# Weight tiles before the MLP split by DMAs on GpSimd's queue, and the RG-LRU's directions summed by a DMA

## The chip, the cores and the metric

The kernel runs on one core of a Trainium2 chip. The metric is the device time of one execution in microseconds. Before the change three runs took 1648.96, 1650.98 and 1652.66 us; the median is 1650.98. The profile was taken of one further execution.

## What is computed

One layer of a hybrid backbone over 1024 latent tokens and 256 context tokens, width 1024, all in float32:

```python
rgx, gate, s5u = split(modulate(x, sh1, sc1) @ w_in)        # [1024, 3 * 1024], context likewise
xc   = centred_dwconv(rgx)                                  # width 4
h_f, h_b = rglru(xc, forward), rglru(xc, backward)          # 8 heads, gates of 128x128, linear scans
rg   = (h_f + h_b) * gelu(gate)
y    = s5(s5u, forward) + s5(s5u, backward) + d * s5u       # 64 groups, complex diagonal state of 64
g    = gelu(y);  s5 = g * sigmoid(g @ glu_w + glu_b)
out  = concat(rg, s5) @ w_out + b_out
x1   = layer_norm(alpha * x + g1 * out)
x2   = layer_norm(alpha * x1 + g2 * (relu(modulate(x1, sh2, sc2) @ w1 + b1) ** 2 @ w2 + b2))
```

The scans of the latents start from the last state of the context's scan in the same direction.

## The kernel before

Channels lie on the 128 partitions and tokens along the free axis. Every float32 product is made of three products of float32r parts: a weight tile `w` and an input `x` are each written as a high and a low part, and PE takes high by high, high by low and low by high. The function `weights` (line 101) makes the parts of one weight tile of 128 x 1024 (512 KB): SP loads the raw tile into a buffer of tag `wr`, ACT casts it to the high part `wh`, and DVE subtracts to get the low part `wl`. Each of the three tags has three buffers. All weights of the two-dimensional products pass through it.

```python
raw = wp.tile([P, 1024], F32, tag="wr", name="wr", bufs=3)
ld(raw, src)
S.copy(hi, raw)
tt(lo, raw, f(hi), SUB)
```

The program is one long straight line in stages, without loops on the chip. `tc` plans the order on every engine's queue beforehand; an engine then works through its queue in order and waits there for what an instruction needs. `after(ins)` puts instructions behind `ins` on an engine's queue.

1. Start. The modulations are computed, the inputs are modulated and split, and the first two tiles of the input projection (`wrg`) are multiplied along with that. The parameters of S5 are computed on DVE.
2. The mixer's inner part, in an order written out by hand as letters: G is a tile of the RG-LRU's input projection (`proj_rgx`), S one of S5's (`proj_s5`), R a head of the RG-LRU (`rg_head`), X and T are S5's matrices (`make_xt`, `s5_taps`). G and S call `project` (line 359), which takes a weight tile and makes 72 products of it. A head convolves a row on DVE (`xc`), ACT rounds it to `xch`, DVE makes `xcl`, PE makes the gates (`ps_g`), ACT takes sigmoid, exponential, tanh and root, and DVE scans both directions. Then DVE adds the backward scan to the forward one, and SP (GpSimd for head 7) stores the sum as `hs`.
3. `s5_in` makes what each chunk of tokens adds to the state. `proj_gate` makes the eight gate tiles: `project`, GELU, load of `hs`, product, store as `mx`. Two scans over the chunks (`scan`) run on DVE as chains of small operations.
4. The first half of the output projection takes the stored tiles `mx` (`mix_in`). For five of them the low part is already made as the change does it for weights: ACT writes the negated high part, and a DMA on GpSimd's queue adds the raw tile to it. `k_outer` multiplies two weight tiles at once, channel by channel, for tiles 0 and 1 and again for 6 and 7; tiles 2 to 5 go one by one through `prod` (48 products a tile).
5. S5's outputs (`s5_out`): ACT and DVE copy the states that the chunks start from (`s5_states`), PE multiplies, ACT takes GELU (`gs`). The GLU has eight weight tiles, the first two in `k_outer` along with `s5_out`, the others one by one. The other modulations (`mods`) are loaded by SP as `mo` and multiplied on DVE here and in the next stage.
6. The second half of the output projection, 16 steps: eight weight tiles for the first 512 tokens, and the same eight again for the others, 24 products a step. SP also loads the partial sum and the input into a `pin` buffer, which shares the tag `wr`. The first norm runs on DVE beside it.
7. The MLP with the second norm. Its weights go through `weights` and `weights2`.

For stages 5 and 6 the raw tiles were asked for two tiles ahead, through the list `ahead` (lines 816 and 958).

Of the kernel before, what the change touches and what calls it, by code (L numbers as in the profile page):

```python
# [15 lines left out]
P = 128  # L16
# [25 lines left out]
def build(nc, tc, a, out):  # L42
# [51 lines left out]
    def split_affine(h, lo, t, x, scale, bias, behind=None):  # L94
        # h + lo = scale * x + bias; t is for the part of it that h leaves
        with after(behind):
            S.activation(h, x, AF.Identity, bias=bias, scale=scale)
        S.activation(t, f(h), AF.Identity, bias=bias, scale=-1.0)
        stt(lo, x, scale, t, MUL, ADD)
# [45 lines left out]
    def mods1(k0, n):  # L145
        # shift and scale of the channel tiles k0 to k0 + n, both of latents and context
# [108 lines left out]
    # lambda to the powers 8, 16, .. 128, as re, im, -im  # L255
# [13 lines left out]
    # softplus(-lambda), times 8  # L269
# [87 lines left out]
    alt = [0]  # L357

    def project(m, ctx, evict, behind=None, load=None):
        wh, wl = weights(a["w_in"][m], load)  # L360
# [17 lines left out]
    # a row of the convolution's input: context at 1, latents at 260, zeros around them  # L378
    RGW = 1 + NC + 2 + 1 + NL + 2

    def proj_rgx(m):
# [8 lines left out]
        if m < 2:  # L390
            for i, ps in enumerate(early[m]):
                evict(i, ps)
        else:
            project(m, True, evict)
# [4 lines left out]
    def rg_head(h, xr):  # L399
# [28 lines left out]
        # a = exp(-s), s = 8 softplus(-lambda) r; 1 - a^2 = tanh(s / 2) (1 + a)^2  # L428
        # (each function for both directions at once: the tables change thrice a head)
# [20 lines left out]
        tt(it[0][:, NC:NT], it[0][:, NC:NT], it[1][:, NC:NT], ADD)  # L450
        d = dr.tile([P, NL], F32, name=f"hs{h}")
        (nc.sync if h < 7 else G).dma_start(out=d, in_=it[0][:, NC:NT])
        hsum[h] = d

# [8 lines left out]
    def proj_s5(m):  # L463
# [8 lines left out]
        project(16 + m, True, evict)  # L472
# [4 lines left out]
    def make_x(g0, n):  # L477
        # X[(d, p), g, (t, ci)]
# [27 lines left out]
    def s5_taps(m):  # L506
# [9 lines left out]
        # tap 0 of both directions and the skip  # L516
# [46 lines left out]

    rxs = [proj_rgx(0), proj_rgx(1)]
    step = {"R": lambda m: rg_head(m, rxs[m]), "G": lambda m: rxs.append(proj_rgx(m)), "S": proj_s5, "X": make_xt, "T": s5_taps}
    for o in ('X0 R0 T0 G2 S0 R1 X1 S1 T1 R2 X2 G3 S2 T2 R3 G4 X3 T3 X4 R4 T4 S3 G5 R5 X5 S4 G6 X6 T5 R6 G7 X7 S5 T6 R7 T7 S6 S7').split():
        step[o[0]](int(o[1:]))
# [30 lines left out]
    def scan(hf):  # L598
        h = H[hf]
        hs = slice(hf * GH, (hf + 1) * GH)  # L600
        # the context's chunks in pairs, pairs of pairs ..: its last state in the last of its chunks
# [21 lines left out]
    def proj_gate(m):  # L623
# [8 lines left out]
        project(8 + m, False, evict, last_in[m] if m else None, in_ld[m - 2] if m >= 2 else None)  # L632
# [42 lines left out]
    def k_outer(ws, xs, tags, name, ks_=range(KT)):  # L675
        # some tiles of a product at once, over the channels as they come
# [16 lines left out]
    for m, pss in enumerate(k_outer([weights(a["w_out"][0, m]) for m in range(2)], mix_next, ("rg", "si"), "ps_wo")):  # L693
        put_part(m, pss)
    for m in range(2, 6):
        w = weights(a["w_out"][0, m])
# [5 lines left out]
    for m, pss in enumerate(k_outer([weights(a["w_out"][0, m]) for m in (6, 7)], lambda k: mix[k], ("rg", "mm"), "ps_wo",  # L702
# [5 lines left out]
    sop.append(pool("so1", stack=sost))  # L708
    wglu = [weights(a["glu"][m]) for m in range(2)]

    def starts(H, h2, g, cp):
        # the states that the chunks start from, in the chunks' own order
# [42 lines left out]
    for hf in range(2):  # L755
# [6 lines left out]
        # their place is that of the states  # L762
# [53 lines left out]
    ahead = [weights(a["glu"][m]) for m in range(2, 2 + 2)]  # L816
    for m in range(8):
        if m > 1:
            if m + 2 < 8:
                ahead.append(weights(a["glu"][m + 2]))  # L820
            w = ahead.pop(0)
# [21 lines left out]
    def mean_of(pl, x, n):  # L843
        # the mean over all channels of tiles whose sum is x, on every partition
# [4 lines left out]
    def rsqrt(v, t):  # L849
        # v to the power -1/2 in t[0], t[1] is taken as well; the engines' roots are refined by a step of Newton's  # L850
# [7 lines left out]
    def rstd_of(pl, n, tag, sq):  # L858
        # 1 / standard deviation on every partition, from the sum of the tiles' squares
# [15 lines left out]
    def normalise(pl, ys, n, tag, done):  # L875
        """ys less their mean over the channels, over their standard deviation, in place; done(m) after each. In steps."""
# [24 lines left out]
    def centre(n):  # L901
        """Tiles, sent in one by one, less their mean over the channels, in place. In steps."""
# [15 lines left out]
    def scale(pl, n, tag, done, end):  # L918
        """Tiles of no mean, sent in one by one, over their standard deviation, in place; done(m) after each. In steps."""
# [38 lines left out]
    ahead = [weights(a["w_out"][1, m]) for m in range(2)]  # L958
    for j in range(2):
        ys = []  # L960
        for m in range(8):
            if 8 * j + m + 2 < 16:
# [260 lines left out]
```

## Time and profile before

| | |
|---|---|
| runs | 1648.96, 1650.98, 1652.66 us, median 1650.98 |
| span of the profiled execution | 1648.7 us (the page gives no other time of its own; it is 2.3 us below the median) |
| PE busy | 1557.3 us, 94% |
| DVE busy | 1109.4 us, 67% |
| ACT busy | 711.3 us, 43% |
| GpSimd (POOL) busy | 8.8 us, 1% |
| bytes moved by DMA | 199.27 MB, 121 GB/s over the span |

Times are in microseconds from the start of the span. An engine is busy while an instruction of its own runs; the profile says of idle time what ended it. A DMA has two times: what its issue takes on the queue, and the time from issue to landing. The DMA share is the mean busy share of the sixteen DMA engines. PEclk is TensorE's granted clock as a share of 2.4 GHz, so 0.50 is 1.2 GHz.

### The profile page before, as it was taken

The numbers are of one execution on the slowest core, as the hardware profiler recorded it, in microseconds if no ns is written. First come the engines' busy times: TensorE is split into PE (matmuls) and PEld (weight loads), VectorE is DVE, ScalarE is ACT, GpSimd is POOL, SyncE is SP. The second block draws the span as 40 slices with busy tenths as digits, with TensorE's granted clock in tenths as the row PEclk, the third lists the DMA queues.
The fourth block names the chain that finished last, engine by engine and source line by source line (L and its number), as shares of the span: only waits on it lengthen the run. The fifth ranks groups of instructions, "written<-read, shape, count | busy, mean of one in ns | idle before, by whom it ended". The sixth has DMA issues, their size and how long they took to land.

```text
span 1648.7 us, 20069 instructions
## 1 busy us (share of the span) xinstructions
PE 1557.3 (94%) x7508; PEld 1271.8 (77%) x7508; DVE 1109.4 (67%) x2371; ACT 711.3 (43%) x978; POOL 8.8 (1%) x37
## 2 busy tenths in 40 slices
PE   7899998999879999799999899999999999999997
PEld 2687777777758787697778688888888888888887
DVE  7999899998939899329878853343432334247856
ACT  4666667666792326744335642113130303031225
POOL 0000000000000100000000000000000000000000
PEclk9999999999999999899999899999999999999998
DMA  8533323333745836965686422112110202022202
GB/s 268 204 118 112 105 104 115 124 115 108 255 151 167 237 132 149 230 166 196 202 280 184 168 86 72 39 39 64 52 52 17 73 13 90 13 77 84 70 1 103
DMA packets 92721, 199.27 MB, mean 121 GB/s; under 512 B 12496, under 2 KB 43728, under 8 KB 91472
## 3 DMA queue, kind: packets, MB, share of 16 engines
q1 hardware_dynamic: 77424, 176.10, 34.1%
q10 hardware_dynamic: 14048, 17.70, 3.1%
q0 software_dynamic: 1152, 4.19, 1.1%
q8 instruction: 59, 0.97, 0.2%
q14 instruction: 38, 0.31, 0.1%
HBM read 153.98 MB, written 43.98 MB: 120 GB/s over the span
## 4 chain that ended last, share of the span: by engine, by line
PE 62%; DVE 19%; DMA 8%; ACT 6%; issue 4%; SPq 0%; ACTq 0%; DVEq 0%; POOLq 0%
PE ps_m L665 22%; PE ps_m L1052 21%; PE ps_g L425 3%; PE ps_mm L370 3%; PE ps_wo L665 3%; DMA mo<-in_ada_t 2%; PE ps_wo L684 2%; DVE xc L56 2%; DVE ii L47 2%; DVE wl L47 2%; ACT H L593 1%; DVE mo L56 1%; PE ps_gl L684 1%; DVE rr L56 1%; DVE ii L445 1%
## 5 line engine op out<-in xcount | busy, mean ns | idle before, releaser
L665 PE MATMUL ps_m<-x,wh 128*128 128x512 f32 x1024 | 324.8, 398 | 7.8 <-DVE yb L47 7.8
L665 PEld LDWEIGHTS ps_m<-x,wh 128*128 128x128 f32 x1024 | 193.8, 189 | 55.9 <-issue 8.4
L1052 PE MATMUL ps_m<-hh,w2h 128*128 128x512 f32 (+1 forms) x576 | 211.3, 368 | 0.0
L1052 PE MATMUL ps_m<-hl,w2h 128*128 128x512 f32 (+1 forms) x576 | 210.9, 366 | 0.0
L1052 PE MATMUL ps_m<-hh,w2l 128*128 128x512 f32 (+1 forms) x576 | 210.9, 366 | 0.0
L665 PE MATMUL ps_m<-x,wl 128*128 128x512 f32 x512 | 204.1, 399 | 0.0
L47 DVE TENSOR_TENSOR acc<-ps_m,acc 128x512 f32<-128x512 f32 (+1 forms) x144 | 90.8, 631 | 141.5 <-PE ps_m L1052 140.7
L90 ACT CAST wh<-wr 128x1024 fp32r<-128x1024 f32 x88 | 92.2, 1051 | 212.9 <-PE ps_m L665 102.5
L47 DVE TENSOR_TENSOR wl<-wr,wh 128x1024 fp32r<-128x1024 f32 x88 | 107.4, 1222 | 106.9 <-ACT wh L90 106.6
L370 PE MATMUL ps_mm<-x0h,wh 128*128 128x512 f32 x352 | 140.5, 399 | 1.0 <-ACT wh L90 1.0
L370 PE MATMUL ps_mm<-x0h,wl 128*128 128x512 f32 x352 | 140.5, 400 | 0.9 <-DVE wl L47 0.9
L370 PE MATMUL ps_mm<-x0l,wh 128*128 128x512 f32 x352 | 140.2, 398 | 0.0
L1034 ACT CAST w2h<-wr 128x1024 fp32r<-128x1024 f32 x28 | 28.7, 1051 | 237.2 <-PE ps_m L1052 206.5
L1052 PEld LDWEIGHTS ps_m<-hh,w2h 128*128 128x128 f32 x576 | 108.6, 189 | 18.4 <-ACT hh L1015 0.6
L1052 PEld LDWEIGHTS ps_m<-hl,w2h 128*128 128x128 f32 x576 | 108.6, 189 | 18.0 <-issue 0.5
L1052 PEld LDWEIGHTS ps_m<-hh,w2l 128*128 128x128 f32 x576 | 108.6, 189 | 17.7 <-issue 0.2
L665 PEld LDWEIGHTS ps_m<-x,wl 128*128 128x128 f32 x512 | 97.0, 189 | 23.8 <-issue 0.2
L47 DVE TENSOR_TENSOR r<-r 128x512 f32<-128x512 f32 x64 | 44.3, 692 | 84.3 <-ACT hh L1015 83.4
L1014 ACT ACTIVATE r<-ps_m,cols 128x512 f32<-128x512 f32 x64 | 43.8, 685 | 99.3 <-PE ps_m L665 91.9
L665 PE MATMUL ps_wo<-ms,wh 128*128 128x512 f32 x256 | 79.9, 392 | 1.6 <-DVE ms L47 1.2
L370 PEld LDWEIGHTS ps_mm<-x0h,wl 128*128 128x128 f32 x352 | 67.3, 191 | 14.4 <-DVE wl L47 1.4
L370 PEld LDWEIGHTS ps_mm<-x0h,wh 128*128 128x128 f32 x352 | 67.2, 191 | 13.6 <-ACT wh L90 1.4
(295 smaller groups left out, 2989.6 us busy)
## 6 DMA issues: line engine op xcount, KB each, us to landing
wr<-in_w SPq DMA_DIRECT2D x64, 512.0 KB, 3.6
mo<-in_ada_t SPq DMA_DIRECT2D x32, 512.0 KB, 4.0
wr<-in_w_in SPq DMA_DIRECT2D x24, 512.0 KB, 4.2
wr<-in_w_out SPq DMA_DIRECT2D x24, 512.0 KB, 4.5
xt<-xt ACTq DMA_DIRECT2D x16, 512.0 KB, 2.7
yd<-Y SPq DMA_DIRECT2D x16, 512.0 KB, 2.6
xt<-xt SPq DMA_DIRECT2D x16, 512.0 KB, 5.2
yf<-yd SPq DMA_DIRECT2D x8, 1024.0 KB, 9.5
```

The lines of the kernel that those rows point to most:

```text
L47: (eng or V).tensor_tensor(out=o, in0=x, in1=y, op=op)
L56: V.scalar_tensor_tensor(out=o, in0=x, scalar=s, in1=y, op0=op0, op1=op1, **kw)
L90: S.copy(hi, raw)
L370: PE.matmul(ps, w[:, ks], x, start=(k == 0 and c == 0), stop=(k == KT - 1 and c == 2))
L425: PE.matmul(ps, w[:, w0:w0 + P], x[:, src:src + n], start=(c == 0), stop=(c == 2))
L445: V.tensor_tensor_scan(out=i, data0=q, data1=i, initial=0.0, op0=MUL, op1=ADD)
L593: S.copy(hv[0:64], ps[0:64])
L665: PE.matmul(ps, u[:, ks], v[:, js], start=(c == 0), stop=(c == 3 * KT - 1))
L684: PE.matmul(ps, u[:, ks], v[:, HS[j]], start=(i == 0 and c == 0), stop=(i == KT - 1 and c == 2))
L1014: S.activation(r, ps, AF.Relu, bias=col("b1", i))
L1034: S.copy(hi, raw)
L1052: PE.matmul(ps, w[:, m * P:(m + 1) * P], x[:, js], start=(c == 0), stop=(c == 3 * bk - 1))
```

## The change

The 54 weight tiles from the third tile of the input projection to the end of the output projection no longer go through `weights`. They stand in one list `wseq` in the order of use. `fetch` loads a tile straight into a high-part buffer by a DMA on GpSimd's queue that casts float32 to float32r. `lower` writes the negated high part on ACT into a low-part buffer and adds the raw tile to that by a second DMA on GpSimd's queue, which reads the tile from HBM again. `take` hands out the next tile and asks for later ones: the low part of the next tile and the high part of the one after it. The high and low parts still have three buffers each. The first two tiles and the MLP's keep `weights`. The forward scan of a head is stored by SP, and a DMA on GpSimd's queue adds the backward scan to it in HBM; DVE's addition is gone.

```diff
+    wseq, whl = [], []
+    def fetch(n):
+        while len(whl) < min(n, len(wseq)):
+            hi = wp.tile([P, 1024], F32R, tag="wh", name="wh", bufs=3)
+            G.dma_start(out=hi, in_=wseq[len(whl)])
+            whl.append([hi, None])
+    lows = [0]
+    def lower(n):
+        while lows[0] < min(n, len(wseq)):
+            i = lows[0]
+            fetch(i + 1)
+            lo = wp.tile([P, 1024], F32R, tag="wl", name="wl", bufs=3)
+            S.activation(lo, f(whl[i][0]), AF.Copy, scale=-1.0)
+            G.dma_start(out=lo, in_=wseq[i], accum_op=ADD)
+            whl[i][1] = lo
+            lows[0] += 1
+    used = [0]
+    def take(ahead=1):
+        i = used[0]
+        used[0] += 1
+        lower(i + 1)
+        fetch(i + 2)
+        lower(i + 1 + ahead)
+        fetch(i + 2 + ahead)
+        return whl[i]
...
-    def project(m, ctx, evict, behind=None, load=None):
-        wh, wl = weights(a["w_in"][m], load)
+    def project(ctx, evict, behind=None):
+        wh, wl = take()
...
-        tt(it[0][:, NC:NT], it[0][:, NC:NT], it[1][:, NC:NT], ADD)
         d = dr.tile([P, NL], F32, name=f"hs{h}")
-        (nc.sync if h < 7 else G).dma_start(out=d, in_=it[0][:, NC:NT])
+        ld(d, it[0][:, NC:NT])
+        G.dma_start(out=d, in_=it[1][:, NC:NT], accum_op=ADD)
...
+    wseq += [a["w_in"][int(o[1:]) + (16 if o[0] == "S" else 0)] for o in order if o[0] in "GS"]
+    wseq += [a["w_in"][8 + m] for m in range(8)] + [a["w_out"][0, m] for m in range(8)]
+    wseq += [a["glu"][m] for m in range(8)] + [a["w_out"][1, m % 8] for m in range(16)]
+    fetch(2)
+    lower(1)
     rxs = [proj_rgx(0), proj_rgx(1)]
...
-    for m, pss in enumerate(k_outer([weights(a["w_out"][0, m]) for m in range(2)], mix_next, ("rg", "si"), "ps_wo")):
+    for m, pss in enumerate(k_outer([take(), take(0)], mix_next, ("rg", "si"), "ps_wo")):
...
-        w = weights(a["w_out"][0, m])
+        w = take()
...
-    wglu = [weights(a["glu"][m]) for m in range(2)]
+    wglu = [take(), take(0)]
...
-            if m + 2 < 8:
-                ahead.append(weights(a["glu"][m + 2]))
-            w = ahead.pop(0)
+            w = take()
...
-            if 8 * j + m + 2 < 16:
-                ahead.append(weights(a["w_out"][1, (m + 2) % 8]))
-            w = ahead.pop(0)
+            w = take()
```

## Rows read from the trace of the kernel before

**Rows 1.** The page: busy time of each engine over the span.
```profile
PE 1557.3 (94%) x7508; PEld 1271.8 (77%) x7508; DVE 1109.4 (67%) x2371; ACT 711.3 (43%) x978; POOL 8.8 (1%) x37
```

**Rows 2.** Windows, stage A and one head: length, engines' busy time, PEclk, DMA share, GB/s.
```profile
core 0: us, PE busy (x) PEld busy (x) DVE busy (x) ACT busy (x) POOL busy (x), PEclk, DMA share, GB/s
153.50:198.00 44.50, 42.18 (x224) 35.11 (x223) 39.40 (x54) 29.16 (x39) 0.17 (x3) 0.96 0.32 110
109.40:410.00 300.60, 281.91 (x1520) 233.65 (x1520) 281.79 (x372) 199.54 (x263) 0.85 (x15) 0.97 0.32 109
```

**Rows 3.** PE's waits, 105 to 412 us: total, times, longest.
```profile
PE ps_g L425 <- ACT xch L411: 13.8, 6, 3.0
```

**Rows 4.** Windows, the chunk scans.
```profile
490.00:640.00 150.00, 144.76 (x620) 118.00 (x620) 141.82 (x705) 46.04 (x59) 4.39 (x5) 0.98 0.54 162
```

**Rows 5.** Tile `wl` on DVE, 490 to 640 us: duration in ns, first and last start.
```profile
L47 DVE TENSOR_TENSOR wl<-wr,wh x15: 1211/1218/1222, 493.4 to 637.6; 128x1024 fp32r<-128x1024 f32 x15
```

**Rows 6.** Timeline of ACT: the first copy of states, and what it waited for.
```profile
637.61 2.09 ACT L714 COPY h<-H 64x1024 f32<-64x1024 f32 x1 [3.93 <-DVE H L47]
```

**Rows 7.** PE's waits, 540 to 700 us.
```profile
PE ps_so L741 <- ACT gs L744: 11.7, 1, 11.7
```

**Rows 8.** Windows, stage F.
```profile
822.00:904.00 82.00, 80.46 (x360) 65.93 (x360) 65.63 (x108) 31.34 (x41) 0.00 (x0) 1.00 0.70 225
```

**Rows 9.** Tile `ms`: stage F's products with the high part of the weights.
```profile
L665 PE MATMUL ps_wo<-ms,wh x256: 387/389/796, 812.4 to 905.9; 128*128 128x512 f32 x128
```

**Rows 10.** DMA, 810 to 908 us: SP's queue (share of 98 us), and loads' time to landing.
```profile
q1 hardware_dynamic: 9502, 21.70, 69.0%
...
wr<-in_w_out SPq DMA_DIRECT2D x12, 512.0 KB, 4.7
```

**Rows 11.** Groups on DVE: the low parts, and the sums of directions.
```profile
L47 DVE TENSOR_TENSOR wl<-wr,wh 128x1024 fp32r<-128x1024 f32 x88 | 107.4, 1222 | 106.9 <-ACT wh L90 106.6
...
L47 DVE TENSOR_TENSOR ii<-ii 128x1024 f32<-128x1024 f32 x8 | 9.8, 1219 | 0.0
```

**Rows 12.** Timeline of SP's queue: start, length, loads of the GLU's first tiles.
```profile
604.91 34.29 SPq L59 DMA_DIRECT2D wr<-in_glu  x4
```

**Rows 13.** Windows, the first outputs of S5.
```profile
640.00:660.00 20.00, 17.47 (x89) 14.32 (x87) 17.57 (x72) 19.87 (x10) 0.00 (x0) 1.00 1.14 223
```

**Rows 14.** Groups on ACT: cast, negation (fourth stage), scaling of `pin`.
```profile
L90 ACT CAST wh<-wr 128x1024 fp32r<-128x1024 f32 x88 | 92.2, 1051 | 212.9 <-PE ps_m L665 102.5 <-DMA wr<-in_w_out 32.5 <-PE ps_gl L665 23.6
...
L971 ACT ACTIVATE pin<-pin,gbc 128x512 f32<-128x512 f32 x16 | 11.5, 722 | 20.0 <-DMA pin<-in_xT 20.0
...
L654 ACT ACTIVATE mh<-mh 128x1024 fp32r<-128x1024 f32 x5 | 5.2, 1056 | 0.1
```

**Rows 15.** Tile `mh`: the adding DMAs' issue in ns, and time to landing.
```profile
L655 POOL DMA_DIRECT2D mh<-mx x5: 862/872/894, 536.4 to 564.8; - x5
...
DMA to landing us min/median/max: 6.3/7.9/11.0
```

**Rows 16.** Tile `hs`: last load, POOL's plain store; its median to landing (DMA issues).
```profile
L59 SPq DMA_DIRECT2D ge<-hs x16: 319/320/424, 415.7 to 559.9; - x16
...
L452 POOL DMA_DIRECT2D hs<-ii x1: 672/672/672, 421.1 to 421.1; - x1
...
hs<-ii POOLq DMA_DIRECT2D x1, 512.0 KB, 5.0
```

**Rows 17.** Windows around a wait of PE.
```profile
568.00:572.00 4.00, 0.66 (x3) 0.22 (x3) 1.91 (x6) 0.00 (x0) 0.00 (x0) 0.87 0.95 227
572.00:576.00 4.00, 4.00 (x10) 3.13 (x11) 1.53 (x4) 1.04 (x1) 0.00 (x0) 0.50 1.04 313
576.00:580.00 4.00, 4.00 (x16) 3.18 (x15) 2.96 (x13) 2.10 (x2) 0.00 (x0) 0.78 0.61 184
```

**Rows 18.** Tiles `G` and `mh`: the GLU's products, the first output projection's.
```profile
L665 PE MATMUL ps_gl<-G,wl x96: 392/397/400, 745.4 to 812.1; 128*128 128x512 f32 x96
...
L665 PE MATMUL ps_wo<-mh,wh x128: 389/389/400, 588.1 to 631.7; 128*128 128x512 f32 x128
```

**Rows 19.** DMA queue of POOL, 545 to 556 us: packets, MB, share.
```profile
q0 software_dynamic: 285, 1.04, 48.6%
```

**Rows 20.** DMA queue of SP in the MLP, 1000 to 1500 us.
```profile
q1 hardware_dynamic: 6803, 24.53, 15.5%
```

More of the change, by code (lines that the diff above doesn't have):

```diff
@@ L393, in proj_rgx @@
         else:
-            project(m, True, evict)
+            project(True, evict)
         return xr
@@ L470, in evict @@
                 S.copy(us[:, :, 0:CC], ps.rearrange("p (c t) -> p t c", t=T8))
-        project(16 + m, True, evict)
+        project(True, evict)
         d = dr.tile([T8, P, NCH], F32, name=f"u{m}")
@@ L562, in s5_taps @@
             st_(kp[rows, 16:128], kt[64:128, 16:128])
+    order = ('X0 R0 T0 G2 S0 R1 X1 S1 T1 R2 X2 G3 S2 T2 R3 G4 X3 T3 X4 R4 T4 S3 G5 R5 X5 S4 G6 X6 T5 R6 G7 X7 S5 T6 R7 T7 S6 S7').split()
+    wseq += [a["w_in"][int(o[1:]) + (16 if o[0] == "S" else 0)] for o in order if o[0] in "GS"]
[3 more added lines that the diff above has]
+    lower(1)
     rxs = [proj_rgx(0), proj_rgx(1)]
     step = {"R": lambda m: rg_head(m, rxs[m]), "G": lambda m: rxs.append(proj_rgx(m)), "S": proj_s5, "X": make_xt, "T": s5_taps}
-    for o in ('X0 R0 T0 G2 S0 R1 X1 S1 T1 R2 X2 G3 S2 T2 R3 G4 X3 T3 X4 R4 T4 S3 G5 R5 X5 S4 G6 X6 T5 R6 G7 X7 S5 T6 R7 T7 S6 S7').split():
+    for o in order:
         step[o[0]](int(o[1:]))
@@ L631, in proj_gate @@
         d = dr.tile([P, NL], F32, name=f"mx{m}")
-        project(8 + m, False, evict, last_in[m] if m else None, in_ld[m - 2] if m >= 2 else None)
+        project(False, evict, last_in[m] if m else None)
         mixs[m] = d
@@ L701, in build @@
         put_part(m, pss)
-    for m, pss in enumerate(k_outer([weights(a["w_out"][0, m]) for m in (6, 7)], lambda k: mix[k], ("rg", "mm"), "ps_wo",
+    for m, pss in enumerate(k_outer([take(), take(0)], lambda k: mix[k], ("rg", "mm"), "ps_wo",
                                     (3, 4, 5, 6, 7, 0, 1, 2))):
@@ L815, in build @@
     g1c, sh2, sc2_, g2c = (mod2[:, 8 * i:8 * i + 8] for i in range(4))
-    ahead = [weights(a["glu"][m]) for m in range(2, 2 + 2)]
     for m in range(8):
         if m > 1:
-            if m + 2 < 8:
-                ahead.append(weights(a["glu"][m + 2]))
-            w = ahead.pop(0)
+            w = take()
         for j in range(2):
@@ L957, in build @@
     steps = iter(())
-    ahead = [weights(a["w_out"][1, m]) for m in range(2)]
     for j in range(2):
```

## The prediction

> **What bounds the kernel now.** I read the page's totals first [rows 1]: PE is busy 1557.3 of 1648.7 us, DVE 1109.4. So all of PE's idle time is 91 us, and since the MLP (from 914 us on) isn't touched, what the change can win lies in PE's waits before it. I looked for those stage by stage.
>
> Stage A, the RG-LRU and S5 order (109 to 410 us, seven heads): over 300.6 us PE is busy 281.9 and DVE 281.8 [rows 2], so both are nearly full and they wait for each other by turns. PE's waits there are 16 us and almost all of one kind: six waits of up to 3.0 us, 13.8 us together, for `xch`, which ACT rounds from the convolution that DVE finishes [rows 3]. The granted clock is 0.96 in a head's window such as the one shown: 4% of PE's rate is lost around those waits. DVE bounds this stage by a little.
>
> Stage D, the end of the chunk scan (490 to 680 us): DVE works 141.8 of the 150 us from 490 to 640 [rows 4] on the two scans, and 15 low parts of weights are taken in between [rows 5]. ACT waits until 637.6 for DVE's last `H` before it can copy states [rows 6], and PE then waits 11.7 us, the longest wait of all, for the `gs` that stands behind those copies on ACT [rows 7].
>
> Stage F, the second half of the output projection (812 to 906 us): PE has no gap worth naming from 822 to 904 (80.5 of 82 us) [rows 8]. Sixteen tiles of 24 products start between 812.4 and 905.9 [rows 9]: 93.5 / 16 = 5.8 us a tile. Here PE alone is the bound; DMA stands at 69% of 98 us [rows 10].
>
> **The change part by part.** *DVE in stage A.* 14 low parts (6 G, 8 S) at 1.222 us and 8 direction sums at 1.219 us [rows 11] go: 26.9 us. PE can give back no more than its idle time, 300.6 - 281.9 = 18.7 us, plus the clock. A head loses two low parts and a sum, 3.7 us, and the wait for `xch` is 2.3 us a head, so I let the six waits go and keep the rest: -12 us. Bounds: 0 (other waits take their place) and -18.7.
>
> *DVE in stage D.* 15 x 1.218 = 18.3 us leave a DVE that is idle only 8.2 of 150, so the scan ends some 15 us sooner and ACT's copies with it. Of PE's 11.7 us, and of the half clock after it, I take -9; the load of `yf` that PE meets next stays. Bounds: -16; and +8, because the GLU's first tiles, loaded by SP from 604.9 to 639.2 in quiet time [rows 12], now wait for high-part buffers that come free at 632 to 654 and so load in the crowd (DMA share 1.14 from 640 to 660 [rows 13]).
>
> *ACT.* The negation replaces the cast one for one: 1056 against 1051 ns [rows 14]; nothing, and behind the same work as the cast.
>
> *SP and POOL.* SP loses 54 loads. POOL gains 54 casting DMAs, 54 adding ones and eight for the sums; an adding DMA occupies it 0.87 us [rows 15], 100 us in all on an engine that is busy 8.8 us [rows 1]. Nothing by itself, but POOL is one queue: an adding DMA waits there for its negation, and the next high part is queued behind it. The sums: head 7's is the nearest to its reader, sent at 421, read at 560 (last `ge` load) [rows 16]; 139 us cover it, without them it would cost one landing, 7.9 us.
>
> *The buffers.* Here is the price. Before, the raw tile waited in its own buffer, and once a `wh` buffer came free only the cast and the subtraction, 1.05 + 1.22 = 2.3 us, were left. Now a tile can't even be fetched until a `wh` buffer (three of them) is free, and then follow a load from POOL, the negation and the adding DMA, all before PE may start it: call this L. With three buffers PE gives two tiles of cover. The casting load has no row: the nearest are a plain 512 KB DMA from POOL, 5.0 us to landing [rows 16], and SP's loads in this very stage, 4.7 [rows 10]; the far one is the adding DMA. I take 5.0, being the same queue and size. The adding DMA has five rows: 6.3 / 7.9 / 11.0 us [rows 15], under DMA shares like those of stage F. So L = 5.0 + 1.06 + 7.9 + 1 (my estimate for ACT's place in line: one `pin` activation of 0.72 us [rows 14] and the hand-overs) = 15.0 us; from below 4.7 + 1.06 + 6.3 = 12.1, from above 11.0 + 1.06 + 11.0 + 1 = 24.
>
> In stage F two tiles are 11.6 us. The shortfall, 3.4 us, is paid once in three tiles, since the three buffers turn together: five times in sixteen tiles, 17 us. After a PE wait of 3.3 us at 568 the granted clock was 0.50 for four us and 0.78 for four more [rows 17], which is 2.9 us of work lost; I take 2.4 for each of the five, 12 us. Stage F: +29. Bounds: +2 (L 12.1, five times 0.5) and +74 (L 24, five times 12.4, plus the clock).
>
> The Trainium skill, *DMA: Bandwidth & Descriptors*, section "Anatomy of one DMA — SWDGE (gpsimd) path", gives such a DMA about 2.0 us plus its bytes at 436 GB/s, an estimate of 3.2 us for 512 KB; by that L would be 8.5 us, no tile would be late, and the sum would be -21. The adding rows above (6.3 at least) disagree with it, so I go by the rows.
>
> *The other two-tile covers.* The GLU has 6 tiles from 745.4 to 812.1, 11.1 us each [rows 18], and the first output projection 4 from 588.1 to 631.7, 10.9 us [rows 18]: two tiles, 22 us, cover L. Only the tile after a pair held at once has one tile of cover, at three places (w_out 3, w_out 7, GLU 3): 15.0 - 11 less the 1.4 us by which the pair's first buffer is free sooner, 2.6 us, a bit less where DMA is calm: +6 for the three. Bounds 0 and +30.
>
> **Sum:** -12 - 9 + 29 + 6 = +14 us on the profiled execution's span of 1648.7, which stands 2.3 us below the median of the runs, 1650.98. So 1665.
>
> **Rivals.** *In time* (the other side): L stays under 11.6 us, say 4.7 + 1 + 5, and stage F sees nothing; 1651 - 12 - 9 = 1630. For it: SP's load rows, and a POOL with nothing else to do. Against it: no adding row lands under 6.3 us, and all of them were issued at most two at a time. It decides at 11.6 us. Chance 0.32, since the cast row is missing and the order that the planner picks on POOL may give more cover than I count. The Trainium skill's figure above would make this the case.
>
> *The DMA engines full:* two adding DMAs took 48.6% of 11 us [rows 19], 2.7 us of all sixteen engines each, against 15.5% of 500 us for 24.53 MB by SP [rows 20], 1.66 us for 512 KB. Stage F would need 0.69 x 98 + 16 x 2.7 = 111 us of engine time in 98, 127 if the cast costs what the adding does. Then every landing stretches, F costs about +45, the covers +10, D +8: 1651 - 12 + 63 = 1702. It decides when F's share reaches 1. Chance 0.12; against it, F's pin and ada loads can wait in part.
>
> *It buys nothing:* DVE's relief in A and D doesn't reach PE (PE is as full as DVE in A) and only +35 remains: 1686. Chance 0.08.
>
> *They cancel* within 0.2% (3.3 us, about what a measurement of this kernel can tell from no change): 0.08.
>
> **How the numbers follow.** The forecast, slower by 4 to 30 us, has 0.40; with the full engines and the empty relief, slower has 0.60, same 0.08, faster 0.32. The range goes from 1628, just below the in-time case, to 1700, just short of the full engines; about 0.12 is left out below and 0.07 above. The forecast alone would be 1655 to 1681. One part of it can be wrong without the rest: the gains in A and D hang on DVE, the loss in F on L.
>
> **What would show it.** In stage A, waits for `xch` of under 5 us and head windows of 41 us or less; in D, `H` done by 625 us and the 11.7 us wait down to a few. In F, PE waits for `wl` by the adding DMA, every third tile, the stage at 115 to 125 us instead of 94, clock below 0.95, landings of the adding DMA at 7 us or more. If `wl` lands before its tile in F, with no PE wait, the forecast is wrong; if the DMA share in F is 1 and SP's pin loads land after 8 us and more, the full engines are the cause.

## The result, and the profile after

The changed kernel takes 1741.08 us (median of four runs) against 1649.97 for the kernel before: ratio 1.0544, 95% interval 1.0524 to 1.0563. Forecast were 1665 and a range up to 1700, so the direction was right and the size was not. The profiled execution's span is 1740.8 us, and the mean granted clock 0.960 against 0.978.

The page's totals, to hold against [rows 1]:

```profile
span 1740.8 us, 20125 instructions
...
PE 1575.4 (90%) x7508; PEld 1283.4 (74%) x7508; DVE 1044.1 (60%) x2309; ACT 709.9 (41%) x978; POOL 93.4 (5%) x152
```

DVE lost 65 us of work and PE lost time all the same: its idle time went from 91 to 165 us, and its busy time rose by 18 although it does the same products, at a lower granted clock. So taking work off DVE was not worth time by itself. The stages, from the first and last starts of PE's groups (us):

| stretch | before | after | difference |
|---|---|---|---|
| start to the first input product | 72.8 | 79.1 | +6.3 |
| heads (to the last tap product) | 333.8 | 338.4 | +4.6 |
| from there to the last gate product | 152.3 | 168.8 | +16.5 |
| to the end of the first output projection | 94.8 | 115.4 | +20.6 |
| S5 outputs and the GLU's first pair | 91.1 | 85.0 | -6.1 |
| the GLU's other six tiles | 67.6 | 70.0 | +2.4 |
| second half of the output projection (stage F) | 93.5 | 149.4 | +55.9 |
| to the MLP, and the MLP | 742.8 | 734.7 | -8.1 |

They add up to the 92.1 us between the spans. The last row's gain isn't the change's: 5.5 us of it lie between stage F's last product and the MLP's first, 8.4 us before and 2.9 after. The border between heads and gates needs care: by the last tap product the changed kernel has already done 36 products of the first gate (some 8 us of work) that stood behind it before, so the heads proper gained about 4 us, and the gates lost about 25.

The group of products that marks stage F, after, to hold against [rows 9], and the stage's window, before and after:

```profile
L706 PE MATMUL ps_wo<-ms,wh x256: 387/389/799, 856.7 to 1006.1; 128*128 128x512 f32 x128
...
812.40:905.90 93.50, 90.39 (x401) 73.53 (x400) 73.72 (x118) 37.28 (x48) 0.00 (x0) 1.00 0.69 220
...
856.70:1006.10 149.40, 105.30 (x401) 81.92 (x400) 72.98 (x123) 43.94 (x57) 20.93 (x29) 0.85 0.85 217
```

Of the 55.9 us, 41 are idle time of PE (149.4 - 105.3 = 44.1 us, against 3.1 in the same stage before) and 15 are the same products at a lower clock (0.85; PE busy 105.3 against 90.4 us). Three stretches of four microseconds after a wait of 5.2 us, which ended at 909.8, show the second part, as [rows 17] did: the granted clock is 0.50 (the lower level, 1.2 GHz) in the first, 0.65 in the second and 1.00 in the third.

```profile
909.00:913.00 4.00, 3.19 (x8) 2.55 (x9) 1.84 (x3) 0.00 (x0) 0.00 (x0) 0.50 1.00 211
913.00:917.00 4.00, 4.00 (x13) 3.22 (x12) 0.00 (x0) 0.39 (x1) 0.00 (x0) 0.65 0.92 334
917.00:921.00 4.00, 4.00 (x19) 3.28 (x18) 2.96 (x5) 1.28 (x2) 1.43 (x2) 1.00 0.35 57
```

PE's waits from 72 to 1010 us: us in total, times, longest.

```profile
PE ps_wo L706 <- DMA wl<-in_w_out: 30.3, 9, 10.1
PE ps_si L632 <- DMA xt<-xt: 15.5, 1, 15.5
PE ps_g L459 <- ACT xch L445: 12.9, 6, 2.6
...
PE ps_wo L706 <- ACT ms L830: 10.7, 1, 10.7
PE ps_so L782 <- ACT gs L785: 9.8, 1, 9.8
PE ps_mm L404 <- ACT ge L667: 9.4, 4, 4.8
PE ps_wo L725 <- ACT pt L712: 8.4, 1, 8.4
PE ps_wo L706 <- ACT pt L712: 7.2, 1, 7.2
```

Besides the late low parts there is a second family of waits: `ms`, `ge`, `pt` come from ACT. What held ACT ahead of `ms` and `ge` stands in its own waits (from 420 us to the MLP) and in its timeline of the gates:

```profile
ACT wl L124 <- DMA wh<-in_w_out: 88.5, 15, 10.0
ACT ms L830 <- DVE mx L47: 52.6, 6, 12.6
ACT wl L124 <- DMA wh<-in_w_in: 36.1, 5, 9.1
```

```profile
519.59 1.06 ACT L124 ACTIVATE wl<-wh 128x1024 fp32r<-128x1024 f32 x1 [8.98 <-DMA wh<-in_w_in]
...
533.01 1.06 ACT L124 ACTIVATE wl<-wh 128x1024 fp32r<-128x1024 f32 x1 [7.44 <-DMA wh<-in_w_in]
...
549.80 1.06 ACT L124 ACTIVATE wl<-wh 128x1024 fp32r<-128x1024 f32 x1 [9.08 <-DMA wh<-in_w_in]
```

The negation stands in ACT's queue for seven to nine microseconds, until a high part has landed, and evictions of PSUM (`ge`, at 520.55 for the first) are queued behind it. With `pt` it is another thing: both of PE's waits for it end with a copy that stands behind ACT's copies of the scan's states, as the second does here:

```profile
678.08 1.92 ACT L756 COPY h<-H 64x1024 f32<-64x1024 f32 x1
680.02 0.58 ACT L712 COPY pt<-ps_wo 128x512 f32<-128x512 f32 x1
```

Before the change those copies began at 637.6 us, 16 us before the projection's last product, and PE waited for no `pt`; now they begin at 654.0, 48 us before it, since PE is late. Why the gates' high part is late is read from POOL's timeline:

```profile
510.52 0.86 POOL L696 DMA_DIRECT2D mh<-mx  x1 [75.72 <-ACT mh L695]
511.14 0.81 POOL L114 DMA_DIRECT2D wh<-in_w_in  x1
521.05 0.88 POOL L125 DMA_DIRECT2D wl<-in_w_in  x1 [9.10 <-ACT wl L124]
525.73 0.86 POOL L696 DMA_DIRECT2D mh<-mx  x1 [3.80 <-ACT ge L667]
526.34 0.81 POOL L114 DMA_DIRECT2D wh<-in_w_in  x1
534.47 0.86 POOL L125 DMA_DIRECT2D wl<-in_w_in  x1 [7.32 <-ACT wl L124]
```

POOL is held at a mixed input's adding DMA (`mh`) whose negation isn't done; the fetch of the next gate's high part is issued 0.6 us behind it, and the adding DMA of that tile eight to ten microseconds later. A round takes 15 us, for a gate whose 48 products take 11. POOL is busy 5% of the span and yet holds tiles back: not by its work, by its order.

The third thing is on DVE, GLU and stage F; before, then after (740 to 906, and 780 to 1000 us):

```profile
DVE mo L56 <- DMA mo<-in_ada_t: 11.7, 10, 2.6
```

```profile
DVE mo L56 <- DMA mo<-in_ada_t: 51.1, 21, 5.6
```

The loads of modulation weights on SP, which the change doesn't touch, land later (median 5.2 us against 4.0), and DVE waits for them in order, with the GLU's outputs (`mx`) queued behind: ACT's 52.6 us for `mx` above are the next link, and PE's wait for `ms` the last. The links act on each other, since a negation can stand behind an `ms` cast that waits for `mx` (868.0 us, behind a wait of 12.3).

### The profile page after: what moved, and what is told of

Same layout as the page of the kernel before. It is cut to its first block, busy times and chain, and to the rows that moved or that the text cites. A ratio compares the mean times of both kernels' runs of the same rounds, so it can differ in the third digit from the quotient of the medians.

```text
span 1740.8 us, 20125 instructions
## 1 busy us (share of the span) xinstructions
PE 1575.4 (90%) x7508; PEld 1283.4 (74%) x7508; DVE 1044.1 (60%) x2309; ACT 709.9 (41%) x978; POOL 93.4 (5%) x152
## 4 chain that ended last, share of the span: by engine, by line
PE 57%; DVE 16%; issue 12%; DMA 7%; ACT 6%; POOL 2%; SPq 0%; ACTq 0%; POOLq 0%; DVEq 0%
PE ps_m L706 21%; PE ps_m L1087 20%; PE ps_mm L404 3%; PE ps_g L459 3%; DVE sT L47 2%; DMA mx<-ge 2%; DVE xc L56 1%; PE ps_gl L725 1%; DVE ii L47 1%; DVE H L47 1%; DVE Y L47 1%; PE ps_wo L725 1%; DVE sU L47 1%; ACT H L634 1%; DVE rr L56 1%
## 5 line engine op out<-in xcount | busy, mean ns | idle before, releaser
L124 ACT ACTIVATE wl<-wh 128x1024 fp32r<-128x1024 f32 x54 | 57.2, 1059 | 167.2 <-DMA wh<-in_w_out 88.5
L1087 PEld LDWEIGHTS ps_m<-hh,w2h 128*128 128x128 f32 x576 | 108.6, 189 | 18.4 <-ACT hh L1050 0.5
L706 PE MATMUL ps_wo<-ms,wh 128*128 128x512 f32 x256 | 88.8, 429 | 14.1 <-ACT ms L830 10.7
L47 DVE TENSOR_TENSOR wl<-wr,wh 128x1024 fp32r<-128x1024 f32 x34 | 41.6, 1224 | 91.8 <-ACT wh L90 91.8
L706 PE MATMUL ps_wo<-ms,wl 128*128 128x512 f32 x128 | 56.1, 438 | 29.4 <-DMA wl<-in_w_out 29.4
```

Source lines behind the costliest of these rows:

```text
L47: (eng or V).tensor_tensor(out=o, in0=x, in1=y, op=op)
L124: S.activation(lo, f(whl[i][0]), AF.Copy, scale=-1.0)
L706: PE.matmul(ps, u[:, ks], v[:, js], start=(c == 0), stop=(c == 3 * KT - 1))
L1087: PE.matmul(ps, w[:, m * P:(m + 1) * P], x[:, js], start=(c == 0), stop=(c == 3 * bk - 1))
```

## The experiments

Three theories. **Cover** (theory 1): a tile's way from a free buffer to its low part is longer than what PE has to do meanwhile, the more so as fetches and adding DMAs share POOL's one queue. **Crowd** (theory 2): the tiles' DMAs slow the modulation loads that DVE waits for, and the GLU's outputs come late. **ScalarE** (theory 3, formed after the first four runs): the negation waits on ACT for a DMA and holds evictions and casts behind it. The runs up to **Both away** are of one execution each, and four of the changed kernel spread over 10 us (1733 to 1743): a few microseconds between them say nothing.

**Stages taken back one by one.** First stage F's 16 tiles alone, back to a load and a split on ACT and DVE:

```diff
+    ahead = [weights(a["w_out"][1, m]) for m in range(2)]
...
-            w = take()
+            if 8 * j + m + 2 < 16:
+                ahead.append(weights(a["w_out"][1, (m + 2) % 8]))
+            w = ahead.pop(0)
```

> Only the 16 weight tiles of the second half of the output projection (stage F) go back to a load by SP, a cast on ACT and a subtraction on DVE, asked for two tiles ahead. Theory 1 (cover: the loss belongs to the stage whose own tiles are split by DMAs, because a tile is fetched only when one of three high-part buffers is free and the two DMAs and the negation follow one another on POOL's queue): stage F falls from 150 us to 95 to 100 us and the kernel to about 1690 us. Theory 2 (crowd: the ada loads, slowed by the doubled weight traffic, hold DVE's queue from the GLU on, and behind DVE the GLU's results, the negations on ACT and POOL are late): the first tiles of stage F still wait for the GLU's results, stage F stays at 110 us or more and the kernel at about 1705 us.

1713.35 us, 28 less; stage F starts its products from 859.3 to 977.1, 118 us, in which `ms` is waited for 13.1 us. That is theory 2's stage (110 us or more), and slower still than its kernel (1705): with its own tiles back the stage still lost 24 us, so something else made those. Theory 1 has the other 32 us of the stage. Then the GLU's eight tiles too (the same edit in the GLU's loop and pair):

> The eight tiles of the GLU and the 16 of stage F go back to load, cast and subtraction. Theory 1 and theory 2 both expect the GLU and stage F as before the change (67 and 94 us) and the kernel at about 1680 us; what then remains above 1650 us belongs to the gate stage and the first half of the output projection (26 and 21 us in the changed kernel), less 5 us won in the heads. If the kernel comes out below 1665 us, those two losses hang on the later stages' tiles and not on their own.

1691.98 us, another 21; stage F takes 100 us, 851.6 to 952.0, against the 94 that both theories had. The GLU's tiles had cost that stage most of what was left.

**Head 7's store.** In the change SP stores all the forward scans; before, POOL stored head 7's.

```diff
-        ld(d, it[0][:, NC:NT])
+        (nc.sync if h < 7 else G).dma_start(out=d, in_=it[0][:, NC:NT])
```

> The changed kernel, but head 7's forward scan is stored by POOL's queue as before the change, instead of by SP's. Theory 1 (SP stands at that store until the scan is done at 427 us, with the loads of ub and xt for the next stage queued behind it): PE's wait of 15.5 us for xt goes to under 4 us and the kernel falls by 10 to 15 us, to about 1728 us. Theory 2 (xt is late because the DMA engines are busier): the wait stays above 10 us and the kernel within 4 us of 1741.

1740.11 us. PE's 15.5 us for `xt` shrink to 4.6 (420 to 600 us), as theory 1 had it, and the kernel gains nothing that shows. In the same products PE now waits 4.6 us for ACT's copies of `H` and 1.9 for `kt` instead, the gates' last product moves only from 586.3 to 583.9, and the next stage takes 120 us instead of 115. So the longest single wait of the page was worth next to nothing.

**The modulation loads left out** (the line with `ld(aw, a["ada_t"][j])` goes, and VectorE multiplies the row `crow`, which is there already, by itself; the modulations' values are left out):

> The changed kernel without the 32 loads of the ada weights in the GLU and in stage F: the 32 products are made on DVE as before, but of a row that is already there. Left out of the computation: the second set of shifts, scales and gates. Theory 1 (cover and POOL's queue): stage F stays at 115 us or more, with PE waiting for low parts, and the kernel falls by 20 to 35 us. Theory 2 (crowd, DVE held by the ada loads): stage F falls to 100 us or less and the kernel by 45 to 55 us, to about 1690.

1708.81 us, 32 less, and stage F takes 121 us, both as theory 1 had it. Yet the wait for `ms` is gone, which only theory 2 has, and 18.4 us for low parts are left of 29.4. So the crowd is real too: two causes in one stage. The edit also takes 32 loads off the DMA engines (adding DMAs in F land after 5.6 us in the median instead of 7.0), so not all of the 28 us in F need be VectorE's wait.

**Negation on GpSimd.**

```diff
-            S.activation(lo, f(whl[i][0]), AF.Copy, scale=-1.0)
+            ts(lo, f(whl[i][0]), -1.0, MUL, eng=G)
```

> The negation goes from ScalarE to GpSimd, so that ScalarE no longer stands at it until a high part has landed; GpSimd then waits at the negation in place of the adding DMA. Theory of the blocked ScalarE: the waits of PE for ge (9.4 us) and for pt (8.4 and 7.2) go, the ms wait of 10.7 halves, and the time falls by 20 to 35 us, to 1706 to 1721. Theory of the loop in GpSimd's queue (a high part is fetched only after the adding DMA of the tile ahead has been issued, and that only after the negation of what has landed): the order of the queue is the same and the step of it is longer by what GpSimd's negation takes over ScalarE's 1.06; the 16 tiles of the second half of the output projection take 149.6 us or more, and the time is 1741 to 1775.

1789.47 us. PE's waits for `ge` fall from 9.4 to 4.3 us and for `pt` from 15.6 to 5.4, as the ScalarE theory said (for `pt` not as it meant it: the 4.9 us one again ends behind copies of states), but those for `wl` rise to 52.3 (11), with a negation that takes 2.84 us there and everything behind it:

```profile
L51 POOL TENSOR_SCALAR wl<-wh x54: 2762/2840/5504, 6.5 to 1037.6; 128x1024 fp32r<-128x1024 f32 x54
```

Both mechanisms exist. Which weighs more this run can't say: sixteen negations longer by 1.78 us are 28 of the 35 us by which stage F grew.

**Fetch before negation.**

```diff
-        fetch(i + 2)
-        lower(i + 1 + ahead)
         fetch(i + 2 + ahead)
+        lower(i + 1 + ahead)
```

> At each tile the fetch of the next high part is issued ahead of the negation and the adding DMA of the tile before it, not behind them. Theory of the loop in GpSimd's queue: fetch, negation and adding DMA of neighbouring tiles overlap more, and the step of the loop is no longer a landing of 6.4 plus a negation of 1.06 plus two issues; the 16 tiles of the second half of the output projection fall from 149.6 us to between 110 and 135, and the time to between 1695 and 1725. Theory of the crowd (modulation loads and the other tiles' traffic set the landings), and theory of the blocked ScalarE: both stay within 8 us of 149.6 and 1741.

1744.21 us, stage F 152 us: no change. It decides nothing either. POOL's timeline shows adding DMAs and fetches in the same succession as in the changed kernel (two adding DMAs, then fetches), so the order on POOL is the planner's and the edit didn't move it.

**Four buffers for high parts, fetched a tile further ahead.**

```diff
-            hi = wp.tile([P, 1024], F32R, tag="wh", name="wh", bufs=3)
+            hi = wp.tile([P, 1024], F32R, tag="wh", name="wh", bufs=4)
...
-        fetch(i + 2 + ahead)
+        fetch(i + 3 + ahead)
```

(with `split` given four and three, and the raw tiles `wr`, `mraw`, `pin` two instead of three)

> Four buffers for high parts in place of three, and each high part fetched one tile further ahead; SBUF is full, so the raw tiles of the split that is left, in the modulation rows and from the MLP on, have two buffers in place of three, which may cost the MLP some microseconds of its own (700 us of it after 1009). Theory of the loop in GpSimd's queue: with a high part in hand the negation never waits for it; ScalarE's waits for high parts (50.1 and 88.5 us) fall to a third, the second half of the output projection takes 105 to 125 us, the gates' stage ends 10 to 20 us earlier than 586, and the time without the MLP's own loss is 1670 to 1705. Theory of the crowd: more transfers at once make each one slower; the second half stays above 135 us and the time above 1725.

1734.48 us. In stage F the low parts are all but in time, and the stage still takes 141 us, which is the crowd's figure (above 135):

```profile
PE ps_wo L706 <- ACT ms L830: 17.3, 2, 9.3
PE ps_rs L910 <- DVE ld L53: 8.1, 1, 8.1
PE ps_mu L884 <- DVE mod L47: 6.8, 1, 6.8
PE ps_wo L706 <- DVE ms L47: 3.8, 2, 3.3
PE ps_wo L706 <- DMA wl<-in_w_out: 3.5, 5, 1.1
```

With the cover mended, what DVE holds comes last: `ms` and the modulation behind the late loads. A cause that is taken away uncovers the next one. From the MLP's first product to the end it took 740 us where the changed kernel takes 732, which the raw buffers explain as said beforehand; this wasn't tried by itself.

**Both away** (that kernel without the modulation loads):

> wh4_wr2_f without the 32 loads of modulation weights behind the GLU (left out: VectorE multiplies an old tile in their place, so the modulations are not the reference's). In wh4_wr2_f alone the second half of the output projection took 141 us with 3.5 us of waits for low parts left, in no_ada alone 121 us with 18.4. Theory that two causes, late weight tiles and late modulation loads that hold VectorE's queue, make up the whole 56 us that this stage lost: with both away it comes back to between 94 and 106 us, and the time is 1675 to 1700. Theory that a third one is at work (the clock, or ScalarE's negations): it stays at 112 us or more, and the time at 1705 or more.

1705.71 us, stage F 109.4 us (852.5 to 961.9), between the two bounds written down. Two causes, with the lighter traffic, make up 40 of the 56 us. Of the 16 left, 7.6 are low parts and 6.6 one wait that ends in ACT's queue, where a root's table load stood behind a `pin` scaling that waited 8.2 us for its load.

**The heads alone**, in four kernels: the 14 input tiles by DMA and the sums too; the same with the first fetch ordered behind the first modulations' last product; the tiles without the sums; the sums without the tiles. Everything else is as before the change, head 7's store included. The edits: `wseq` holds the 14 tiles only, `project` gets `w = weights(...)` for gates, and the later stages load and split as before; `with after(lastmod[0]): fetch(1)`; `tt(it[0]..., ADD)` back in place of the second line below; and these two lines in the kernel before.

```diff
-        tt(it[0][:, NC:NT], it[0][:, NC:NT], it[1][:, NC:NT], ADD)
+        G.dma_start(out=d, in_=it[1][:, NC:NT], accum_op=ADD)
```

> High parts by the casting DMA and low parts by the adding DMA for the 14 input-projection tiles of the head stage alone; gates, output projection and GLU split on ScalarE and VectorE as before the change; the directions summed by DMA, with head 7's forward scan stored by GpSimd's queue. Theory that the whole loss lies in the stages where a tile has only one or two tiles of cover (gates, output projection, GLU): the loss of 91 us goes, and what is left is the head stage's gain of 5 less the 6.5 lost at the start, and a part of the 6 gained at the chunk scan's end: 1642 to 1654. Theory that adding DMAs and the sums by DMA cost wherever they stand: 1660 or more.

> As inner_only, with the first high part's fetch ordered after the last product of the first modulations, so that it is not issued at 1.3 us among the loads that these products wait for. Theory that the start's 6.5 us are this crowding: the first input-projection product comes back from 79 to between 72 and 75 us, and the time is 3 to 7 us below inner_only's, 1636 to 1649. Theory that the start's loss comes of something else (the order that the planner gives the first instructions): within 2 us of inner_only.

> As inner_only, but the two directions are summed on VectorE as before the change, eight sums of 1.2 us. Theory that VectorE bounds the head stage: these 9.8 us come back in part, 3 to 8 us above inner_only. Theory that TensorE bounds it (busy 287 of 305 us there in the kernel before), and that the sums were hidden: within 2 us of inner_only.

> The kernel before with the sum of the directions by an adding DMA alone, stores as before. Theory that VectorE bounds the head stage: 3 to 8 us faster than before, 1642 to 1647. Theory that TensorE bounds it: within 2 us of 1650.

| kernel | us | ratio to before | 95% |
|---|---|---|---|
| inner_only | 1658.86 | 1.0055 | 1.0039 to 1.0071 |
| inner_late | 1658.11 | 1.0057 | 1.0045 to 1.0069 |
| inner_w_only | 1659.08 | 1.0068 | 1.0051 to 1.0086 |
| sum_only_h7 | 1650.48 | 1.0005 | 0.9993 to 1.0017 |

The sums by DMA are worth nothing, and the DMA split of the 14 tiles makes the kernel 9 us slower. It doesn't lose them in the heads: PE waits there for no weight tile, and the stretch (337.0 us against 333.8) holds the 36 gate products as well, so that some 5 us are gained. In the profiled execution, 5.1 us longer than the one before, the start takes 2.7 us more, the gates, which should be 8 shorter, only 1.5 less, and stage F 3.8 more. What makes them late stays open; with the change the planner orders every queue anew. DVE does 294 us in the heads of inner_only instead of 316, and PE waits as before, six times for `xch`:

```profile
PE ps_g L459 <- ACT xch L445: 12.7, 6, 2.4
```

The start's theory fell: inner_late's first input product comes at 80.6 us, later still, with the same wait of 7.4 us for a modulation load, and sum_only_h7, without any early fetch, starts 3 us late too. Perhaps it goes with the planner's order; it wasn't followed further.

**Each other stage alone**, added to inner_only (the stage's tiles enter `wseq` just ahead of it):

> inner_only (1658.9 us) with the 16 tiles of the second half of the output projection by the two DMAs as well, and nothing else: gates, first output projection and GLU stay split on ScalarE and VectorE. Theory of the prediction (a tile's way of 15 us against a cover of two tiles): 94 to 97 us of stage become 118 to 128, the time 1683 to 1692. Theory of the loop in GpSimd's queue (fetch, negation, adding DMA and the next fetch one after the other, some 9 us a tile): 140 us or more, the time 1705 or more, without any help of the GLU's tiles. Theory that the stage is slow because the GLU before it, by the same DMAs, hands its outputs over late: under 105 us, the time under 1668.

> inner_only with the eight gate tiles by the two DMAs as well. f_glu_back, which has these and the first output projection so, stands 33 us above inner_only. Theory that the gates' tiles lose by GpSimd's queue, in which they stand behind the adding DMAs of the mixed inputs that need the gates before them: 15 to 25 us above inner_only, and the gates end at 575 to 588 us. Theory that the first output projection makes the loss: within 5 us of inner_only.

> inner_only with the eight tiles of the first output projection by the two DMAs as well, fetched from the last gate on. Theory of the negation that holds ScalarE (waits for pt of 8.4 and 7.2 us in the changed kernel): this projection takes 10 to 20 us more than inner_only's 95.5, and the time is 8 to 20 us above inner_only. Theory that only the gates lose, and that the projection was late because its inputs were: within 5 us of inner_only.

> inner_only (1658.9 us) with the eight GLU tiles by the two DMAs as well. Theory of the prediction (a GLU tile has 11 us, two tiles cover its way, only the tile after the pair is late): 2 to 6 us above inner_only. Theory that the negations hold ScalarE, whose casts of the GLU's outputs then come late to the second half of the output projection: 10 to 25 us above inner_only, most of it as waits for ms in that half.

> inner_only with the GLU's eight tiles and the 16 of the second half of the output projection by the two DMAs. If the losses add, the time is inner_only's and the 32.7 us that only_f has over it and what only_glu has over it. Theory that they feed each other (GLU tiles in GpSimd's queue hold the first fetches of the second half, and late outputs hold the negations): 10 us or more above that sum, and the second half takes 145 us or more against only_f's 135.7.

Each against before on its own chip, and over inner_only (+9.6). The last row is of one run, and the GLU's time has the widest interval, 1.0146 to 1.0214 of before:

| tiles by DMA, beside the 14 | us | before there | over inner_only |
|---|---|---|---|
| gates | 1669.45 | 1650.39 | +9.5 |
| first output projection | 1662.27 | 1650.39 | +2.3 |
| GLU | 1679.77 | 1648.63 | +21.5 |
| stage F | 1691.57 | 1650.39 | +31.6 |
| GLU and stage F | 1710.83 | 1648.63 | +52.6 |
| gates and first output projection (f_glu_back, one run) | 1691.98 | 1654.31 | +28.1 |

GLU and stage F add (21.5 + 31.6 = 53.1): glu_f's theory of mutual harm falls, though its stage F takes 148.7 us, since the GLU alone already lengthens that stage. Gates and first output projection do not add: 28.1 together, 11.8 one by one. So the 91 us are about 10 for the 14 tiles of the heads, 28 for these two, 21 for the GLU and 32 for stage F. The stages show why two don't add. The first output projection alone takes 13 us longer (566.9 to 675.1, 11.8 of it waits for `pt`), but the S5 outputs behind it, which wait for ACT's copies anyway, take 9.9 us less than before the change. With the gates alone they take 10.1 less, and with both 10.9: however late PE comes, that wait can be saved only once. Part of it isn't saved at all but met earlier, as waits for `pt` behind the copies of states.

Stage F alone takes 135.7 us, more than the prediction's theory had (118 to 128) and less than the loop's (140), and its waits show the prediction's own term beside one that it lacked:

```profile
PE ps_wo L707 <- DMA wl<-in_w_out: 16.8, 7, 4.7
PE ps_wo L707 <- ACT ms L831: 7.9, 1, 7.9
PE ps_rs L914 <- DVE ld L53: 4.0, 1, 4.0
```

And PE from 655 to 945 us, in inner_only, then with the GLU's tiles too:

```profile
PE ps_so L783 <- ACT gs L786: 10.3, 1, 10.3
...
PE ps_wo L707 <- ACT ms L831: 3.1, 1, 3.1
```

```profile
PE ps_so L784 <- ACT gs L787: 19.8, 1, 19.8
PE ps_wo L707 <- ACT ms L832: 13.4, 2, 9.0
```

No GLU tile is late. The loss is ahead of the GLU and behind it: 5.5 us in the S5 outputs and the pair, where ACT's timeline shows the pair's negation waiting 4.0 us for its high part with `gs` right behind,

```profile
685.54 1.06 ACT L124 ACTIVATE wl<-wh 128x1024 fp32r<-128x1024 f32 x1 [4.00 <-DMA wh<-in_glu]
686.51 1.06 ACT L787 ACTIVATE gs<-ps_so 128x512 f32<-128x512 f32 x2
```

and 20.9 us in stage F, which waits for the GLU's outputs and takes 118 us with its own tiles on SP. What makes those outputs late is DVE's queue: it waits 29.9 us for modulation loads, and 14.2 in inner_only (740 to 920 us).

```profile
DVE mo L56 <- DMA mo<-in_ada_t: 14.2, 13, 2.6
```

```profile
DVE mo L56 <- DMA mo<-in_ada_t: 29.9, 18, 3.6
DVE G L47 <- ACT G L795: 14.3, 2, 10.5
```

The second row is ACT's lateness reaching DVE (3.8 us in inner_only). Which of the two sets stage F's loss wasn't tried. No kernel of these beats the one before; sum_only_h7 equals it.

## Why the prediction was right in direction and wrong in size

It had +14 us on the span, and +92.1 came. Of the 78 us between them, stage F has 27, the gates and the first output projection 41 (with the 8 us of gate work put to the gates), the heads and stage D 11, the start 6, the GLU's six tiles all but nothing; only the 8 behind stage F go the other way. So one term was of the wrong size, and two that were put at nothing, ACT's wait and POOL's order, stand behind much of the rest.

**Stage F: right mechanism, half the size.** The step "L = 15 us against two tiles' 11.6" held. Landings in F were 7.1 us for the casting load and 7.0 for the adding DMA (medians, changed kernel): 7.1 + 1.06 + 7.0 + 1 = 16.2. Once the GLU was through, long waits for a low part came at 909.8, 934.6 and 965.3 us (the first two three tiles apart, as said), of 5.2, 5.4 and 10.1 us instead of 3.4. Alone (only_f) they sum to 16.8 us where the working had 17. That is partly luck: they are seven waits of 0.2 to 4.7 us where the working had five of 3.4, and by 16.2 us it would have had five of 4.6. The loading price was taken too low (5.0 for 7.1) and the adding price too high (7.9 for 7.0), and these nearly cancelled. By the Trainium skill, *DMA: Bandwidth & Descriptors*, "Anatomy of one DMA — SWDGE (gpsimd) path", 3.2 us was the estimate for either; the runs disagree by a factor of two.

The step that failed in F is that only its own tiles were priced. 14 us of its idle time are waits for `ms` (10.7 from ACT, 3.3 from DVE), outputs of the GLU that are late because DVE waits in order for modulation loads. The prediction had F's pin and ada loads "can wait in part" and left it there; on whose queue they would be waited for was not asked. The clock took 15 us where 12 were reckoned.

**"Two tiles, 22 us, cover L", for the GLU.** True of its tiles, and they cost 21.5 us, in the stages around it. Two steps failed: the ada loads on DVE's queue, as above, and *ACT*, "nothing, and behind the same work as the cast". The negation was priced by its duration, which held (1.06 us). What changed is what it waits for: the cast read a raw tile that had been in SBUF for long; the negation reads a tile whose fetch has just been issued, and ACT stands there with evictions queued behind. The changed kernel's `ge` and 4.0 us of only_glu's `gs` are that wait in the rows above; `pt` is ACT's queue too, but there it is the copies of states that stand ahead.

**SP and POOL, "nothing by itself".** The same sentence named the mechanism (the next high part queued behind an adding DMA that waits for its negation) and gave it no price. In the gates it is the stage's rhythm: `mh`, fetch, nine microseconds, adding DMA. The gates were in no sum at all, and the first output projection only with a late tile or two; together they cost 28 us. How the 28 divide between POOL's order and ACT's wait is argued from the timelines and wasn't tried.

**Stage A: -12 was forecast, about -4 came**, and a kernel with the DMA split there alone is 9 us slower, with a start that was in no sum. "I let the six waits go" failed: the six waits for `xch` are still 12.9 us. What DVE got back it spent for the most part waiting for ACT's `ii`, the gate that it multiplies before it scans (78 to 385 us, before, then after):

```profile
L47 DVE TENSOR_TENSOR ii<-ii,xc 128x256 f32<-128x256 f32 (+1 forms) x28 | 23.0, 822 | 4.5 <-ACT ii L427 4.5
```

```profile
L47 DVE TENSOR_TENSOR ii<-ii,xc 128x256 f32<-128x256 f32 (+1 forms) x28 | 23.0, 821 | 16.2 <-ACT ii L461 16.2
```

So a head is a round over PE, ACT and DVE, and the work taken off DVE was for the most part not what the round lasted by; which of its steps set it stays open. That was the rival "it buys nothing", at 0.08.

**Stage D: -9 was forecast, -6 came, by luck.** PE's wait for `gs` is 9.8 instead of 11.7 us: the first scan's last `H` released ACT at 654.0 us, not at 637.6 and not by 625, and by then PE itself was late. What DVE was spared, it waited for ACT (430 to 660 us): 12.1 us for `ge` instead of 1.5, and 9.0 for ACT's part of `H` instead of 0.9. The 6 us are the wait that is saved once.

**"The DMA engines full" did not happen by its own sign**: the DMA share in F is 0.85, and SP's `pin` loads there land after 6.4 us in the median, not 8. POOL's queue took 52.8% of 149 us for 16.23 MB there, 2.5 us of all sixteen engines for 512 KB, where the prediction had 2.7. Over the stage, then, throughput was left. But the share isn't even (1.00 and 0.92 from 909 to 917 us above, 0.35 in the four after), and how far full stretches made the landings late wasn't tried.

**Head 7's store on SP** was missed. It made PE's longest single wait and cost nothing that could be measured.

## What to carry to other kernels

When an operation is swapped for one of the same length on the same engine, price its new wait: what it now waits for, and everything queued behind it on an in-order engine. Splitting weights by DMA puts three steps in series (fetch, negate, add) with a buffer held all the way, so it needs a cover of the whole way, about 16 us here. And cover is not enough: the GLU's tiles had it, none was late, and the loss came from what stood behind the negation and from loads that the added traffic slowed. Relief of a busy engine pays only where the work taken away is what the next engine waits for: here the engine spent it waiting for another. And a long wait in the list need not be worth its length, as taking away the 15.5 us one showed.

## What was not expected of the hardware

The landing times of POOL's 512 KB DMAs spread widely: casting 3.7 / 6.4 / 13.9 us and adding 5.1 / 6.9 / 12.0 (min, median, max, changed kernel, the two rows below). PE's longest wait for a low part, 10.1 us, is twice what the medians in stage F leave (16.2 less 11.6 us of cover, 4.6). A negation of a 128x1024 tile took 2.84 us on GpSimd against 1.06 on ScalarE.

```profile
DMA to landing us min/median/max: 3.7/6.4/13.9
```

```profile
DMA to landing us min/median/max: 5.1/6.9/12.0
```
